# An encoder block on one core: the feed-forward norm's normed blocks in buffers apart from the squares, the squares taken by 256 columns into PSUM, and the first norm's weight loaded between the blocks

## The chip, the cores and the metric

The kernel runs on one core of a Trainium2 chip. The metric is the device time of one execution in microseconds (us), as the median of several. TensorE (PE) multiplies matrices and transposes, VectorE (DVE) and ScalarE (ACT) work element by element, GpSimd (POOL) issues the gathers of table rows and some loads, and SyncE (SP) issues nearly all other transfers. PSUM holds the results of PE, SBUF the tiles. A tile made with `bufs=N` has N buffers in turn: the N+1st waits until the first is no longer needed.

## The reference

One layer over 1024 tokens of width 1024:

```python
def rms_norm(x, g):
    y = x * lax.rsqrt(jnp.mean(x * x, axis=-1, keepdims=True) + EPS)
    return y * g

h = rms_norm(x, mix_norm_g)                    # "first norm"
proj = h @ w_in                                # u, q, k, v, f_logit, g_ssm, g_att
merged = sigmoid(g_ssm) * s5_branch(u, ...) + sigmoid(g_att) * forgetting_attention(q, k, v, f_logit, ...)
x = x + merged @ w_out                         # output projection and residual
h2 = rms_norm(x, ffn_norm_g)                   # "feed-forward norm"
x = x + peer_ffn(h2, w_query, sub_keys, u_tab, v_tab)
```

`peer_ffn` makes queries from `h2` (8 heads of 256), finds the best experts among 16384 by two sets of 128 keys, and mixes the experts' rows `u` and `v` by gates.

## The kernel before, in words

The tokens are worked on in two groups of 512 (group 0, group 1), each in NB = 4 blocks of 128. For each group the function that the diff touches does, in turn: the first norm (L470 to L489), the forget gate (weight `wf`, L496 to L507), the projections (`unit` gets a weight in two halves as `ws`; `by_token`, L460, and `by_column`, L466, multiply), the two branches, and the part named `mix` (from L822): the output projection with the residual (L838), the feed-forward norm (L843 to L851), and then the query heads (L866 on: `w_query` units with L466, keys `sk`, scores L881).

The feed-forward norm goes like this before the change. The residual L838 writes a block's 1024 columns in four strokes of 256, each from one of two PSUM banks `mm`; the strokes of one quarter of the columns come for all four blocks, then the next quarter. When a block is whole, it is stored to `d_x` (L843) and ACT squares its 1024 columns at once into a tile `sq` with two buffers, while it sums them into `ms` (L845). `inverse_root` (L431, then L150 to L155: twelve small DVE instructions with the constants) works on two blocks at a time. L850 writes the normed block, and its tile is again named `sq`: squares and normed blocks share the same two buffers. The normed block is stored to `d_h` (L851) and turned by `transposed`: eight PE transposes (L171) in two halves, each of which ACT copies (L173) and DVE splits (L174) into `h2T`. So a third normed block can be written only when the store of the first has landed.

A scheduler that simulates the engines sets each engine's order of instructions from the program; the rows below show it as it came out. Work of the next or the former part is laid in between: in group 0 the feed-forward norm stands directly ahead of group 1's first norm (its `hT`) and forget gate, and `h2T` of group 0 is stored to `d_hT` (L864, 3 MB). In group 1 the norm is followed by the loads `dhT` on POOL, the query heads, and the dense part (L1127 on, L1148 and L1208), in which all experts' rows are streamed. Ahead of group 1's norm the same engines gather expert rows for a first part of the tokens (`r`, L995, with DVE's L1001 and L1003).

SP works through its queue in order. It holds eight semaphores for landings in turn, so that a transfer there is issued only when the one eight places before it has landed.

Of the kernel before, what the change touches and what calls it, by code (L numbers as in the profile page):

```python
# [20 lines left out]
FT = mybir.dt.float32  # L21
# [4 lines left out]
AF = mybir.ActivationFunctionType  # L26
OP = mybir.AluOpType
AX = mybir.AxisListType.X
DVE, PE = mybir.EngineType.DVE, mybir.EngineType.PE

S = 1024
D = 1024
P = 128
# [24 lines left out]
def kernel(ctx: ExitStack, tc: tile.TileContext, x, w_in, w_f, w_query, w_out, w_glu,  # L58
                      g_mix, g_ffn, q_g, k_g, f_bias, a_re, a_im, log_step, b_re, b_im, c_re, c_im,
                      d_skip, sub_keys, uv, ut, out):  # L60
    nc = tc.nc
    const = ctx.enter_context(tc.tile_pool(name="const", bufs=1))
    dram = ctx.enter_context(tc.tile_pool(name="dram", bufs=1, space=bass.MemoryType.DRAM))
    psum = ctx.enter_context(tc.tile_pool(name="psum", bufs=1, space=bass.MemoryType.PSUM))
# [26 lines left out]
    def row_bcast(pool, name, src, n, parts=P):  # L91
        t = pool.tile([parts, n], FT, name=name)
        nc.sync.dma_start(t, bass.AP(tensor=src.tensor, offset=src.offset, ap=[[0, parts], [1, n]]))
        return t
# [327 lines left out]
    def front(g):  # L422
        t0, GT = GROUPS[g]
        NB, NC, B0 = GT // P, GT // L, t0 // P
# [5 lines left out]
        def inverse_root(pool, o, m):  # L430
            nc.vector.tensor_scalar(m, m, 1.0 / D, EPS, op0=OP.mult, op1=OP.add)  # L431
            rsqrt(pool, o, m)
# [38 lines left out]
        with tc.tile_pool(name=f"nrm{g}", bufs=1, side="right", reuse_waits="tile") as sp:  # L471
            xs = []
            ms = sp.tile([P, NB], FT, name="ms")
            rs = sp.tile([P, NB], FT, name="rs")
            for b in range(NB):
                xb = sp.tile([P, D], FT, name="xb", bufs=NB)
                nc.sync.dma_start(xb, x[t0 + b * P:t0 + (b + 1) * P, :])
                sq = sp.tile([P, D], FT, name="sq", bufs=NB)
                nc.scalar.activation(sq, xb, AF.Square, accum_out=ms[:, b:b + 1])
                xs.append(xb)  # L480
            gmix = row_bcast(sp, "gmix", g_mix, D)
            if g == 0:
                load_constants()
            for b in range(NB):
                if b % 2 == 0:
                    inverse_root(sp, rs[:, b:b + 2], ms[:, b:b + 2])
                hb = sp.tile([P, D], FT, name="sq", bufs=NB)
                nc.vector.scalar_tensor_tensor(hb, xs[b], rs[:, b:b + 1], gmix, op0=OP.mult, op1=OP.mult)
                transposed(hT[:, :, :, b * P:(b + 1) * P], hb)  # L489
# [120 lines left out]
        sp = ap_ctx.enter_context(tc.tile_pool(name=f"att{g}", bufs=1, side="left", reuse_waits="tile"))  # L610
# [10 lines left out]
        for hp in range(4):  # L621
# [6 lines left out]
            rs = pj.tile([P, 2, NB, 2], FT, name="rs", bufs=2)  # L628
            for qk in range(2):
                w = unit(w_in[2 + 4 * qk + hp], "att")  # L630
                raw = pj.tile([P, NB, 2, P], FT, name="qkraw", bufs=2)
                for b in range(NB):
# [3 lines left out]
                    for h in range(2):  # L636
                        sq = pj.tile([P, P], FT, name="sq")
# [184 lines left out]
        with tc.tile_pool(name=f"mix{g}", bufs=1, side="left", reuse_waits="tile") as sp:  # L822
            h2T = sp.tile([P, 8, 2, GT], FR, name="h2T")
            nx = ExitStack()
            mp = nx.enter_context(tc.tile_pool(name=f"res{g}", bufs=1, side="left", reuse_waits="tile"))
            gffn = row_bcast(mp, "gffn", g_ffn, D)
            xs = []
            for b in range(NB):
                xb = mp.tile([P, D], FT, name="xb", bufs=NB)
                nc.sync.dma_start(xb, x[t0 + b * P:t0 + (b + 1) * P, :])  # L830
                xs.append(xb)
            for q in range(4):
                w = unit(w_out[q], "out")
                cs = slice(q * 256, (q + 1) * 256)
                for b in range(NB):
                    pp = mm_bank([P, 256])
                    by_token(pp, mT, w, b, 0)
                    nc.vector.scalar_tensor_tensor(xs[b][:, cs], pp, 0.25, xs[b][:, cs],  # L838
                                                   op0=OP.mult, op1=OP.add)
            ms = mp.tile([P, NB], FT, name="ms")  # L840
            rs = mp.tile([P, NB], FT, name="rs")
            for b in range(NB):
                nc.sync.dma_start(d_x[B0 + b], xs[b])  # L843
                sq = mp.tile([P, D], FT, name="sq", bufs=2)
                nc.scalar.activation(sq, xs[b], AF.Square, accum_out=ms[:, b:b + 1])  # L845
            for b in range(NB):
                if b % 2 == 0:
                    inverse_root(mp, rs[:, b:b + 2], ms[:, b:b + 2])
                hb = mp.tile([P, D], FT, name="sq", bufs=2)
                nc.vector.scalar_tensor_tensor(hb, xs[b], rs[:, b:b + 1], gffn, op0=OP.mult, op1=OP.mult)  # L850
                nc.sync.dma_start(d_h[B0 + b], hb)  # L851
                pump(*BESIDE["norm"])
                transposed(h2T[:, :, :, b * P:(b + 1) * P], hb)
            if last_group:
                pump(0, 1000)
                gates_ctx.close()
                apart_ctx.close()
            nx.close()
            sp = nx.enter_context(tc.tile_pool(name=f"query{g}", bufs=1, side="left", reuse_waits="tile"))
            tops = [sp.tile([P, 2, H, 2, 16], FT, name="tops", bufs=NB) for _ in range(NB)]  # L860
            if last_group:
                dense_input(h2T)
            else:
                nc.sync.dma_start(d_hT, h2T[:, :, :, N1:].bitcast(FT))  # L864
            yield
            for h in range(H):  # L866
                w = unit(w_query[h], "mix")
                sk = sp.tile([P, 2, P], FT, name="sk", bufs=2)
                nc.sync.dma_start(sk, sub_keys[:, 2 * h:2 * h + 2, :])
                qs = []  # L870
                for c in range(2):
                    pq = mm_bank([P, GT])
                    by_column(pq, h2T, w, c)
                    q = sp.tile([P, GT], FT, name="q", bufs=2)
                    nc.scalar.activation(q, pq, AF.Copy)
                    qs.append(q)
                for b in range(0, NB, 2):
                    pc = tp_bank([P, 2, 2, P])
                    for bb in range(2):
                        for c in range(2):  # L880
                            nc.tensor.matmul(pc[:, bb, c, :], qs[c][:, (b + bb) * P:(b + bb + 1) * P],  # L881
                                             sk[:, c, :], start=True, stop=True)
                    sc = sp.tile([P, 2, 2, P], FT, name="sc", bufs=2)
                    nc.scalar.activation(sc, pc, AF.Copy)
                    for bb in range(2):
                        top = tops[b + bb]
                        for c in range(2):
                            top16(sc[:, bb, c, :], top[:, 0, h, c, :], top[:, 1, h, c, :].bitcast(U32))
            for b in range(NB):
                nc.sync.dma_start(d_s[B0 + b], tops[b])  # L890
            nx.close()
# [426 lines left out]
```

## Time and profile before

| | us |
|---|---|
| median of the runs | 3397.88 |
| the runs | 3397.88, 3392.59, 3992.58 |
| the profiled execution, its own time | 3395.97 |
| its span in the trace | 3394.0 |
| PE busy in the span | 3209.4 (95%) |
| DVE busy | 2587.1 (76%) |
| ACT busy | 1220.3 (36%) |
| POOL busy | 1032.7 (30%) |

The span is what the trace covers; the execution's own time is 1.97 us longer. The run of 3992.58 stands apart from the other two. The page of the profile also gives the chain of work that ended last, followed back from the last instruction: PE is 78% of it, DVE and DMA 7% each. The mean granted clock of TensorE in the profiled execution was 0.972 of full speed.

### The profile page before, as it was taken

The numbers are of one execution on the slowest core, as the hardware profiler recorded it, in microseconds if no ns is written. First come the engines' busy times: TensorE is split into PE (matmuls) and PEld (weight loads), VectorE is DVE, ScalarE is ACT, GpSimd is POOL, SyncE is SP. The second block draws the span as 40 slices with busy tenths as digits, with TensorE's granted clock in tenths as the row PEclk, the third lists the DMA queues.
The fourth block names the chain that finished last, engine by engine and source line by source line (L and its number), as shares of the span: only waits on it lengthen the run. The fifth ranks groups of instructions, "written<-read, shape, count | busy, mean of one in ns | idle before, by whom it ended". The sixth has DMA issues, their size and how long they took to land.

```text
span 3394.0 us, 51977 instructions
## 1 busy us (share of the span) xinstructions
PE 3209.4 (95%) x18959; PEld 2859.5 (84%) x18959; DVE 2587.1 (76%) x5405; ACT 1220.3 (36%) x2693; POOL 1032.7 (30%) x831
## 2 busy tenths in 40 slices
PE   7899998979999797799999999999999999999998
PEld 6788777867788686789999998988888889889887
DVE  7645454788877657578898788888988888897987
ACT  4444242323455444313774222222222222222221
POOL 0000000002222022200213365555545555564643
PEclk9999898989999998899999999999999999999999
DMA  7877996756577599945979798989989899898996
GB/s 253 284 266 278 295 330 238 278 202 227 184 227 240 137 325 336 324 175 173 256 217 320 273 362 295 348 316 333 337 309 365 323 333 345 311 348 298 359 328 230
DMA packets 465312, 965.42 MB, mean 284 GB/s; under 512 B 198304, under 2 KB 226208, under 8 KB 440480
## 3 DMA queue, kind: packets, MB, share of 16 engines
q1 hardware_dynamic: 345872, 545.43, 47.0%
q0 software_dynamic: 119184, 416.67, 34.3%
q8 instruction: 149, 2.44, 0.3%
q14 instruction: 107, 0.88, 0.1%
HBM read 775.84 MB, written 186.12 MB: 283 GB/s over the span
## 4 chain that ended last, share of the span: by engine, by line
PE 78%; DVE 7%; DMA 7%; issue 4%; ACT 2%; POOL 1%; SPq 0%; DVEq 0%; ACTq 0%; POOLq 0%
PE mm L1148 25%; PE S L1208 20%; PE mm L460 9%; PE mm L466 7%; PE tp L1208 5%; PE tp L1096 3%; PE S L692 2%; PE S L727 2%; PE S L696 1%; DMA wraw<-in_w_in_dram 1%; PE S L466 1%; POOL r L995 1%; PE tp L719 1%; DMA d_h<-sq 1%; DMA sw<-d_sc 1%
## 5 line engine op out<-in xcount | busy, mean ns | idle before, releaser
L1148 PE MATMUL mm<-dhT,us 128*128 128x320 f32 x6144 | 976.8, 310 | 5.1 <-ACT ag L1150 2.2
L1148 PEld LDWEIGHTS mm<-dhT,us 128*128 128x128 f32 x6144 | 930.3, 188 | 32.8 <-ACT ag L1150 2.6
L1208 PE MATMUL S<-vs,w 128*128 128x512 f32 x3072 | 794.0, 393 | 0.9 <-ACT vs L1205 0.9
L995 POOL DMA_INDIRECT r<-in_uv_dram,idx x384 | 481.4, 1254 | 783.4 <-DVE dots L1003 410.7
L995 POOL DMA_INDIRECT r<-in_uv_dram,second x384 | 515.6, 1343 | 602.2 <-DVE acc L1001 433.7
L1208 PEld LDWEIGHTS S<-vs,w 128*128 128x128 f32 x3072 | 565.7, 188 | 106.2 <-ACT vs L1205 1.9
L460 PE MATMUL mm<-ws,hT 128*128 128x256 f32 x3456 | 463.4, 292 | 49.1 <-ACT qkraw L635 24.2
L1001 DVE SCALAR_TENSOR_TENSOR acc<-r,dots,acc 128x1024 f32<-128x1024 f32 x384 | 492.0, 1281 | 18.9 <-DMA r<-in_uv_dram,second 17.2
L1003 DVE CUSTOM_DVE_ANT_0 r<-r,h 128x1024 f32<-128x1024 f32 x384 | 466.1, 1221 | 33.3 <-DMA r<-in_uv_dram,idx 32.6
L460 PEld LDWEIGHTS mm<-ws,hT 128*128 128x128 f32 x3456 | 439.5, 198 | 61.0 <-ACT qkraw L635 26.9
L1205 ACT ACTIVATE vs<-vraw 128x512 fp32r<-128x512 f32 x256 | 160.2, 627 | 351.5 <-DMA vraw<-in_uv_dram 226.9
L1140 ACT ACTIVATE us<-uraw 128x512 fp32r<-128x512 f32 x256 | 160.1, 627 | 304.5 <-PE mm L1148 282.3
L1208 PE MATMUL tp<-vs,w 128*128 128x512 f32 x768 | 259.5, 391 | 2.9 <-ACT vs L1205 2.9
L1141 DVE TENSOR_TENSOR us<-uraw,us 128x512 fp32r<-128x512 f32 x256 | 175.5, 687 | 100.4 <-ACT us L1140 100.1
L1150 ACT ACTIVATE ag<-mm 128x320 f32<-128x320 f32 x256 | 111.2, 435 | 347.4 <-PE mm L1148 343.5
L673 POOL DMA_DIRECT2D rk<-d_ck x16 | 9.4, 587 | 704.4 <-DVE tops L161 353.7
L1206 DVE TENSOR_TENSOR vs<-vraw,vs 128x512 fp32r<-128x512 f32 x256 | 175.6, 688 | 58.5 <-ACT vs L1205 58.3
L1082 ACT ACTIVATE two<-two,eT 128x128 f32<-128x128 f32 x640 | 201.7, 393 | 44.7 <-DVE two L1079 44.4
L466 PE MATMUL mm<-h2T,ws 128*128 128x512 f32 x768 | 183.0, 394 | 0.2 <-ACT h2T L173 0.2
L1096 PE MATMUL tp<-one,two 128*128 128x128 f32 x1280 | 172.8, 281 | 7.7 <-ACT two L1082 7.4
L1096 PEld LDWEIGHTS tp<-one,two 128*128 128x128 f32 x1280 | 164.3, 194 | 13.1 <-ACT two L1082 8.4
L1208 PEld LDWEIGHTS tp<-vs,w 128*128 128x128 f32 x768 | 143.5, 188 | 33.1 <-ACT vs L1205 3.3
(310 smaller groups left out, 3728.1 us busy)
## 6 DMA issues: line engine op xcount, KB each, us to landing
d_w<-ws SPq DMA_DIRECT2D x76, 1024.0 KB
ws<-d_w SPq DMA_DIRECT2D x76, 1024.0 KB
uraw<-in_ut_dram SPq DMA_DIRECT2D x256, 256.0 KB
vraw<-in_uv_dram SPq DMA_DIRECT2D x256, 256.0 KB
gs<-d_g SPq DMA_DIRECT2D x32, 1280.0 KB
d_g<-sg SPq DMA_DIRECT2D x40, 960.0 KB
wraw<-in_w_in_dram SPq DMA_DIRECT2D x44, 512.0 KB
d_a<-ag SPq DMA_DIRECT2D x32, 320.0 KB
```

What stands on the lines that cost most here:

```text
L460: nc.tensor.matmul(o, act[:, k, i, b * P:(b + 1) * P], w[k // 4][:, k % 4, j, :], start=(n == 0), stop=(n == 23))
L466: nc.tensor.matmul(o, w[k // 4][:, k % 4, i, c * P:(c + 1) * P], act[:, k, j, :], start=(n == 0), stop=(n == 3 * kk - 1))
L995: nc.gpsimd.indirect_dma_start(out=r, out_offset=None, in_=halves, in_offset=bass.IndirectOffsetOnAxis(ap=at, axis=0))
L1001: nc.vector.scalar_tensor_tensor(acc, r, dots[:, k:k + 1], acc, op0=OP.mult, op1=OP.add)
L1003: nc.vector.tensor_tensor_reduce(r, r, h2, 1.0, 0.0, op0=OP.mult, op1=OP.add, accum_out=dots[:, k:k + 1])
L1082: nc.scalar.activation(two[:, t, :], two[:, t, :], AF.Copy, scale=eT[:, 2, t1 + t:t1 + t + 1])
L1096: nc.tensor.matmul(pg[:, t, :], two[:, t, :], one[:, t, :], start=True, stop=True)
L1141: nc.vector.tensor_sub(us[:, :, 1, :], raw, us[:, :, 0, :])
L1148: nc.tensor.matmul(pa, parts[k // 4][:, k % 4, i, :], hT[:, k, j, ts], start=(n == 0), stop=(n == 23))
L1205: nc.scalar.activation(vs[:, 0, :], raw, AF.Copy)
L1206: nc.vector.tensor_sub(vs[:, 1, :], raw, vs[:, 0, :])
L1208: nc.tensor.matmul(out_of[b], w[:, p, b * P:(b + 1) * P], vs[:, q, :], start=(i == 0 and p == q), stop=(i == C8 - 1 and q == 1))
```

## The change

The squares get a PSUM tile `S` of 256 columns with two buffers, and are taken after each stroke of the residual, with their sums into `part` (four per block), which a DVE reduction adds up for two blocks. The normed blocks get three buffers of their own, `hb`; the fourth takes the next buffer of `xb`, that of the group's block 0 after its store to `d_x`. In the first norm the weight `gmix` is loaded after the second block and no longer after the fourth.

```diff
--- before.py
+++ after.py
@@ -475,10 +475,11 @@
             for b in range(NB):
                 xb = sp.tile([P, D], FT, name="xb", bufs=NB)
                 nc.sync.dma_start(xb, x[t0 + b * P:t0 + (b + 1) * P, :])
+                if b == 1:
+                    gmix = row_bcast(sp, "gmix", g_mix, D)
                 sq = sp.tile([P, D], FT, name="sq", bufs=NB)
                 nc.scalar.activation(sq, xb, AF.Square, accum_out=ms[:, b:b + 1])
                 xs.append(xb)
-            gmix = row_bcast(sp, "gmix", g_mix, D)
             if g == 0:
                 load_constants()
             for b in range(NB):
@@ -829,6 +830,9 @@
                 xb = mp.tile([P, D], FT, name="xb", bufs=NB)
                 nc.sync.dma_start(xb, x[t0 + b * P:t0 + (b + 1) * P, :])
                 xs.append(xb)
+            ms = mp.tile([P, NB], FT, name="ms")
+            rs = mp.tile([P, NB], FT, name="rs")
+            part = mp.tile([P, NB, 4], FT, name="part")
             for q in range(4):
                 w = unit(w_out[q], "out")
                 cs = slice(q * 256, (q + 1) * 256)
@@ -837,16 +841,15 @@
                     by_token(pp, mT, w, b, 0)
                     nc.vector.scalar_tensor_tensor(xs[b][:, cs], pp, 0.25, xs[b][:, cs],
                                                    op0=OP.mult, op1=OP.add)
-            ms = mp.tile([P, NB], FT, name="ms")
-            rs = mp.tile([P, NB], FT, name="rs")
+                    sq = psum.tile([P, 256], FT, name="S", bufs=2)
+                    nc.scalar.activation(sq, xs[b][:, cs], AF.Square, accum_out=part[:, b, q:q + 1])
             for b in range(NB):
                 nc.sync.dma_start(d_x[B0 + b], xs[b])
-                sq = mp.tile([P, D], FT, name="sq", bufs=2)
-                nc.scalar.activation(sq, xs[b], AF.Square, accum_out=ms[:, b:b + 1])
             for b in range(NB):
                 if b % 2 == 0:
+                    nc.vector.tensor_reduce(ms[:, b:b + 2], part[:, b:b + 2], axis=AX, op=OP.add)
                     inverse_root(mp, rs[:, b:b + 2], ms[:, b:b + 2])
-                hb = mp.tile([P, D], FT, name="sq", bufs=2)
+                hb = mp.tile([P, D], FT, name="hb", bufs=3) if b < 3 else mp.tile([P, D], FT, name="xb", bufs=NB)
                 nc.vector.scalar_tensor_tensor(hb, xs[b], rs[:, b:b + 1], gffn, op0=OP.mult, op1=OP.mult)
                 nc.sync.dma_start(d_h[B0 + b], hb)
                 pump(*BESIDE["norm"])
```

The lines of the changed kernel are counted on by these edits: L838 becomes L842, L843 L847, L850 L853, L851 L854, L864 L867, L496 L497, L869 L872.

On SP, in group 0, where the feed-forward norm ends; `wf` is the forget gate's weight of group 1, `sk` the first keys. Before:

```order
L843 DMA d_x_124<-xb 128x1024
L851 DMA d_h_129<-sq 128x1024
L851 DMA d_h_130<-sq 128x1024
L851 DMA d_h_131<-sq 128x1024
L851 DMA d_h_132<-sq 128x1024
L496 DMA wf<-in_w_f_dram 128x64
L869 DMA sk<-in_sub_keys_dram 128x256 x2
L864 DMA d_hT<-h2T 2048x1x384
L527 DMA d_ck<-rows 8x512 x2
```

After the change:

```order
L854 DMA d_h_129<-hb 128x1024
L854 DMA d_h_130<-hb 128x1024
L847 DMA d_x_124<-xb 128x1024
L854 DMA d_h_131<-hb 128x1024
L854 DMA d_h_132<-xb 128x1024
L867 DMA d_hT<-h2T 2048x1x384
L497 DMA wf<-in_w_f_dram 128x64
L872 DMA sk<-in_sub_keys_dram 128x256 x2
L528 DMA d_ck<-rows 8x512 x2
```

The store of `d_hT` now stands ahead of the load of `wf` and of `sk`, and the first two normed blocks are stored ahead of the last `d_x`.

On DVE, in group 1, around the last stroke of the residual (`mm` to `xb`). Before:

```order
L154 TENSOR_TENSOR rsq_t<-rsq_t,ms 128x2
L155 SCALAR_TENSOR_TENSOR rs<-rsq_t,rs 128x2
L838 SCALAR_TENSOR_TENSOR xb<-mm,xb 128x256
L850 SCALAR_TENSOR_TENSOR sq<-xb,rs,gffn 128x1024 x2
L431 TENSOR_SCALAR ms<-ms 128x2
L150 TENSOR_SCALAR rs<-ms 128x2
L174 TENSOR_TENSOR h2T<-tp,h2T 128x4x128
L153 SCALAR_TENSOR_TENSOR rsq_t<-rs 128x2
L174 TENSOR_TENSOR h2T<-tp,h2T 128x4x128
```

After the change, in the same place:

```order
L154 TENSOR_TENSOR rsq_t<-rsq_t,ms 128x2
L842 SCALAR_TENSOR_TENSOR xb<-mm,xb 128x256
L155 SCALAR_TENSOR_TENSOR rs<-rsq_t,rs 128x2
L853 SCALAR_TENSOR_TENSOR hb<-xb,rs,gffn 128x1024 x2
L842 SCALAR_TENSOR_TENSOR xb<-mm,xb 128x256
L174 TENSOR_TENSOR h2T<-tp,h2T 128x4x128
L850 TENSOR_REDUCE ms<-part 128x2
L431 TENSOR_SCALAR ms<-ms 128x2
L174 TENSOR_TENSOR h2T<-tp,h2T 128x4x128
```

The first two normed blocks now come ahead of the last stroke, and the sum of the second two blocks' squares stands behind the first split of `h2T`.

On SP, in group 1, in the same place of the program; the `ws` rows are halves of `w_query`'s units. Before:

```order
L453 DMA ws<-d_w_6294 128x2048
L453 DMA ws<-d_w_6301 128x2048
L843 DMA d_x_128<-xb 128x1024
L851 DMA d_h_133<-sq 128x1024
L851 DMA d_h_134<-sq 128x1024
L851 DMA d_h_135<-sq 128x1024
L851 DMA d_h_136<-sq 128x1024
L453 DMA ws<-d_w_6418 128x2048
L453 DMA ws<-d_w_6425 128x2048
L869 DMA sk<-in_sub_keys_dram 128x256 x2
```

After the change:

```order
L854 DMA d_h_133<-hb 128x1024
L453 DMA ws<-d_w_6321 128x2048
L453 DMA ws<-d_w_6328 128x2048
L854 DMA d_h_134<-hb 128x1024
L847 DMA d_x_128<-xb 128x1024
L854 DMA d_h_135<-hb 128x1024
L854 DMA d_h_136<-xb 128x1024
L453 DMA ws<-d_w_6445 128x2048
L453 DMA ws<-d_w_6452 128x2048
L872 DMA sk<-in_sub_keys_dram 128x256 x2
```

The first normed block's store moved ahead of a weight's two halves; the weight of the third unit and the keys stand behind all four stores, as before.

## Rows read from the trace of the kernel before

**Rows 1.** The page: busy time by engine, then the chain that ended last

```profile
PE 3209.4 (95%) x18959; PEld 2859.5 (84%) x18959; DVE 2587.1 (76%) x5405; ACT 1220.3 (36%) x2693; POOL 1032.7 (30%) x831
...
PE mm L1148 25%; PE S L1208 20%; PE mm L460 9%; PE mm L466 7%; PE tp L1208 5%; PE tp L1096 3%; PE S L692 2%; PE S L727 2%; PE S L696 1%; DMA wraw<-in_w_in_dram 1%; PE S L466 1%; POOL r L995 1%; PE tp L719 1%; DMA d_h<-sq 1%; DMA sw<-d_sc 1%
```

**Rows 2.** What PE waited for in 1575 to 3394: total us, times, longest

```profile
PE tp L1208 <- ACT vs L1205: 2.9, 1, 2.9
```

**Rows 3.** The chain that ended last, 1 to 30: start, us, what

```profile
2.60 7.82 DMA gmix<-in_g_mix_dram
...
10.75 4.10 DMA wraw<-in_w_in_dram
```

**Rows 4.** Timeline there, ACT: start, us, line, tile, idle before

```profile
14.87 1.06 ACT L447 ACTIVATE ws<-wraw 128x1024 fp32r<-128x1024 f32 x1 [3.64 <-DMA wraw<-in_w_in_dram]
```

**Rows 5.** Timeline of DVE in group 1's feed-forward norm

```profile
1411.74 0.69 DVE L174 TENSOR_TENSOR h2T<-tp,h2T 128x512 fp32r<-128x512 f32 x1
...
1412.54 0.16 DVE L154 TENSOR_TENSOR rsq_t<-rsq_t,ms 128x2 f32<-128x2 f32 x1
1412.73 0.16 DVE L155 SCALAR_TENSOR_TENSOR rs<-rsq_t,rs 128x2 f32<-128x2 f32 x1
1424.55 1.28 DVE L850 SCALAR_TENSOR_TENSOR sq<-xb,rs,gffn 128x1024 f32<-128x1024 f32 x1 [11.66 <-DMA d_h<-sq]
```

**Rows 6.** Timeline of PE in the same place

```profile
1406.87 1.09 PE L171 MATMUL tp<-idf,sq 128*128 128x128 f32 x8 [1.71 <-DVE sq L850]
...
1425.98 1.94 PE L171 MATMUL tp<-idf,sq 128*128 128x128 f32 x8 [14.91 <-DVE sq L850]
...
1430.29 21.41 PE L466 MATMUL mm<-h2T,ws 128*128 128x512 f32 x92 [0.22 <-ACT h2T L173]
```

**Rows 7.** Timeline of SyncE's queue in the same place

```profile
1412.60 15.40 SPq L851 DMA_DIRECT2D d_h<-sq  x4
1440.85 1.23 SPq L453 DMA_DIRECT2D ws<-d_w  x2
1442.17 1.51 SPq L869 DMA_DIRECT2D sk<-in_sub_keys_dram  x2
```

**Rows 8.** Stretches: busy us of PE, PEld, DVE, ACT, POOL; clock, DMA share, GB/s

```profile
560.00:568.00 8.00, 7.31 (x29) 5.28 (x28) 4.43 (x7) 3.58 (x6) 0.00 (x0) 0.50 1.03 369
...
1424.00:1436.00 12.00, 9.24 (x40) 7.23 (x41) 5.24 (x6) 2.28 (x4) 0.00 (x0) 0.77 1.30 390
1436.00:1449.00 13.00, 13.00 (x59) 10.78 (x58) 0.00 (x0) 1.20 (x2) 2.69 (x3) 1.00 1.23 360
1449.00:1452.00 3.00, 3.00 (x17) 2.53 (x17) 0.00 (x0) 0.00 (x0) 0.00 (x0) 1.00 0.20 70
```

**Rows 9.** Timeline of DVE in group 0's feed-forward norm

```profile
545.46 0.69 DVE L174 TENSOR_TENSOR h2T<-tp,h2T 128x512 fp32r<-128x512 f32 x1
...
550.67 2.48 DVE L850 SCALAR_TENSOR_TENSOR sq<-xb,rs,gffn 128x1024 f32<-128x1024 f32 x2 [4.06 <-DMA d_h<-sq]
```

**Rows 10.** Timeline of PE in the same place

```profile
540.40 1.06 PE L171 MATMUL tp<-idf,sq 128*128 128x128 f32 x8 [1.80 <-DVE sq L850]
...
566.15 0.78 PE L504 MATMUL mm<-hT,wfs 128*8 128x512 f32 x1
```

**Rows 11.** Timeline of SyncE's queue in the same place

```profile
558.17 0.58 SPq L864 DMA_DIRECT2D d_hT<-h2T  x1
```

**Rows 12.** Timeline of DVE, then of PE, where group 1's output projection begins

```profile
1347.11 1.28 DVE L1001 SCALAR_TENSOR_TENSOR acc<-r,dots,acc 128x1024 f32<-128x1024 f32 x1 [1.39 <-DMA r<-in_uv_dram,second]
...
1348.79 3.57 PE L460 MATMUL mm<-ws,hT 128*128 128x256 f32 x15 [8.60 <-DVE xb L838]
```

**Rows 13.** Groups of one line: ns min/median/max, first and last start

```profile
L845 ACT ACTIVATE sq<-xb x8: 1049/1058/1062, 530.5 to 1405.7; 128x1024 f32<-128x1024 f32 x8
L845 ACT ACTIVATION_READ_ACCUMULATOR sq<-xb x8: 184/186/193, 531.4 to 1406.7; 128x1 f32 x8
...
L537 ACT ACTIVATE ut<-mm x16: 357/383/385, 37.8 to 600.9; 128x256 f32<-128x256 f32 x16
```

## The prediction

> **What bounds the kernel now.** I read the page first. PE is busy 95% of the span, and the chain that ended last is mostly PE [rows 1]. The dense part at its end (L1148, L1208) has nothing to lose or win here: from 1575 us on PE's longest wait is 2.9 us [rows 2]. So a microsecond won or lost ahead of it passes to the end, and the question is where PE waits in the places that the change touches. There are four: the start, the feed-forward norm of group 0, the first residual of group 1, and its norm. For each I took the timelines of PE, DVE and SP's queue.
>
> In group 1's norm PE stands idle 14.91 us until the third normed block, and DVE in turn waits 11.66 us for the landing of the first block's store `d_h`, because their buffers are shared [rows 5, 6]. The store was issued at 1412.60 [rows 7], when DMA was saturated: it moves 390 and 360 GB/s up to 1449, and 70 after [rows 8]. In group 0 the same wait is only 4.06 us [rows 9]. In both norms PE also waits for the first normed block, 1.71 and 1.80 us [rows 6, 10].
>
> **The start: 0.** `gmix` is the fifth transfer in the queue before; it lands at 2.60 + 7.82 = 10.42 us, and the first norm has its first normed blocks soon after [rows 3]. After the change it is the third, and these are ready some 2.4 us sooner. But ACT's copies of the transposed blocks stand behind the first `ws` copy, which waits until 14.87 for a weight issued at 10.75 [rows 3, 4], in the changed order too. That weight is issued when the fifth transfer has landed, whichever of the five that is, and the five carry the same bytes. So the sooner block waits for the same weight: 0, with bounds of −1 (slower) and +1.5.
>
> **Squares by 256 columns: 0.** Four ACT squares of 1.06 us with a sum read of 0.19, 5.0 us per group, become sixteen. For one of 256 columns the nearest row is L537, 0.38, from PSUM to SBUF; 16 × (0.38 + 0.19) = 9.1 us [rows 13]. The added 4.1 us lie beside the matmuls of the residual, on an engine that is busy 36% [rows 1]. On the path lie only the last square and a reduction of 8 sums, some 0.2 us by the small DVE instructions [rows 5], in place of the whole 1.06 + 0.19; both are inside the next two terms. If ACT had no room the cost would be 4.1 a group.
>
> **Group 1's norm: 12.8, of which 1.5 is lost again.** The sums of the first two blocks no longer wait for a square of 1024 columns, and the order puts both of their normed blocks ahead of the last stroke of the residual. So PE's 1.71 us wait [rows 6] goes, and everything up to the last split of block 1 comes that much sooner: it ended at 1411.74 + 0.69 and now at 1410.72. Behind it stand five small DVE instructions of the second root, 0.19 apart [rows 5]: 0.97. The third normed block then starts at 1411.7, where it started at 1424.55: 12.85 sooner. It needs no store any more. The fourth, 1.28 later, writes the `xb` buffer of block 0, whose `d_x` store must have landed. That holds: the first `d_h` was issued at 1412.60 [rows 7], it stands eight places behind this store in SP's queue before, and a transfer is issued when the one eight before it has landed. Behind the normed blocks the chain is the same, so the first L466 goes from 1430.29 [rows 6] to 1417.5.
>
> What is late next: the third unit's weight and the keys. Their buffers come free with the matmuls of the first unit, so they are issued 12.8 sooner too, at 1428.0 where it was 1440.85 [rows 7]. They are needed when 96 matmuls of L466 are done. These take 21.41/92 = 0.233 each [rows 6], 22.4 together: at 1439.9. They are 2.36 MB (two halves of 1024 KB, two keys of 128 KB). From 1428 to 1449 the trace moves 8 × 390 + 13 × 360 GB/s = 7.8 MB [rows 8], these among them, the rest mainly POOL's loads and gathers. If the two queues share evenly, the weight takes 2 × 2.36 MB at 375 GB/s = 12.6 us and lands at 1440.6, with some 0.8 until PE sees it 1441.4: a loss of 1.5. If it came before all else it would lose nothing; behind all else it lands at 1449 and loses 9.1. I take 1.5, because `d_h`, which the order puts behind another weight's two halves, had landed 11.9 us after its issue [rows 5, 7], though DMA was as full there.
>
> The Trainium skill ("DMA: Bandwidth & Descriptors", section "Queues, rings and completion order") says that each engine goes round between the queue rows that have work, a packet at a time. By that rule the weight can't come behind all else: the sum would keep the 11.3, and without it 3.7 in the worst case. No row here separates the shares of the two queues.
>
> **Group 0's norm: 2.8.** By the same steps PE's 1.80 us [rows 10] go, and the last split of block 1 ends at 545.46 + 0.69 − 1.80 = 544.35. Seven small instructions (1.36) follow in the new order; the third normed block starts at 545.7 instead of 550.67 [rows 9], 5.0 sooner. It would bring L504 from 566.15 [rows 10] to 561.2, if `hT` were the last to come. But the order moves the load of `wf` behind the 3 MB store `d_hT` on SP, and L504 reads it. That store was issued at 558.17 [rows 11], and now at 553.2. At 369 GB/s [rows 8] its 3.15 MB take 8.5 us; with one us from issue to flow it is through at 562.7. Small loads behind big ones in this queue come out after them: `gmix` took 7.82 us behind four blocks [rows 3]. With the split of `wf`, 0.6 us for ACT and DVE together, L504 starts at 563.3: 2.8 sooner. The bounds are 0, if store and load take longer beside the `d_h` stores, and 5.0, if `wf` isn't held up.
>
> The Trainium skill ("DMA: Bandwidth & Descriptors", section "Two DMAs through the same engine are not ordered") says that in one queue of one engine transfers start in order, though they need not end so. By it `wf` would start when the store's last pieces have started, 2.8; without it, 5.0. The landing of `gmix` agrees with it.
>
> **The first residual of group 1: 1.0.** PE waits 8.60 us for the first L838, which stands behind a gather step L1001; that one waited 1.39 us for its row and takes 1.28 [rows 12]. In the new order the first two L838 stand ahead of it. All of it would be 2.7, but the gathers that depend on L1001 come later by as much, and the order of the gathers before is changed a little. I take 1.0, bounds 0 and 2.7.
>
> **The sum.** 0 + 0 + (12.8 − 1.5) + 2.8 + 1.0 = 15.1 us. The profiled execution took 3395.97, 1.9 below the median of 3397.88, so I forecast 3395.97 − 15.1 = 3381 us, 0.5% less. A measurement of this kernel can tell about 2% (68 us) from no change; all cases lie well within. With the terms at moderate ends this case runs from 3376 to 3387. Chance 0.50.
>
> **Rivals.** *The DMA backlog takes most of it back.* The weight and keys land only when the backlog is through: 12.8 − 9.1 + 2.8 + 1.0 = 7.5, so 3388.5. For it speaks that DMA runs full from 1424 to 1449 [rows 8]; against it, that the load is issued 12.8 us sooner. Chance 0.22.
>
> *Everything comes free.* `wf` isn't held up, the weight comes in time, L1001 costs its whole 2.7: 12.8 + 5.0 + 2.7 = 20.5, so 3375.5. Chance 0.12.
>
> *The change doesn't do what it says.* The wait moves to another buffer: the fourth block waits for the store of `d_x` as the third did for `d_h`, and group 1 wins nothing. 2.8 + 1.0 remain: 3392. The issue at 1412.60 speaks against it. Chance 0.08.
>
> *Slower.* The scheduler laid the gathers ahead of group 1's norm a little differently. There DVE and POOL go hand in hand, and a step that meets a row not yet landed stops PE for as much as the 8.60 us seen at 1340 to 1349 [rows 12]. Two more such waits, 17.2, undo the gain (3398); from the second on it is slower, and three give 3395.97 − 15.1 + 25.8 = 3407. Against it: the number of gathers and their order on POOL hardly differ. Chance 0.08.
>
> **How the numbers follow.** The range has to reach from the case with everything free, less the 1.5 of the start and a few us between executions, to the case in which group 1 wins nothing: 3371 to 3394. Left out are the slower case and the edges. No case comes near 2% either way, so "within 2%" has 0.98, and 0.01 for each side.
>
> **What would show it.** In the profile after, group 1's third normed block should start near 1411.7 + the shift so far, with no wait for `d_h`, L466 some 12.8 us sooner beside it, and a new wait of PE at L881 or L466 for the keys or the weight of 1 or 2 us (9 in the first rival). In group 0 L504 should wait for `wfs`. Squares on ACT should take 0.38 us or less. The first L504 should be at 28.4 as before. Wrong would make it a long wait in the gathers, a fourth block that waits for `d_x`, or a keys' landing past 1445.

## The result and the profile after

The changed kernel takes 3378.76 us (median of 8 executions, 3372.07 to 3382.76), the kernel before 3400.32 beside it; the ratio is 0.9942, with a 95% interval of 0.9931 to 0.9952, so 16 to 23 us less of 3400 (the two medians alone give 0.9937, which lies in the interval). The forecast was 3381, the range 3371 to 3394. The profiled execution took 3382.74 us with a span of 3380.8, and lies among the slower of its eight; that of the kernel before took 3395.97 and lies among its faster ones. The two traces are therefore only 13.2 us apart; a second pair of traced executions (3391.44 and 3381.50) is 9.9 apart.

DVE's timeline in the norm of group 1, after the change (start, us, line, tile, idle before); it answers to [rows 5]:

```profile
1398.44 2.48 DVE L853 SCALAR_TENSOR_TENSOR hb<-xb,rs,gffn 128x1024 f32<-128x1024 f32 x2
...
1404.81 0.69 DVE L174 TENSOR_TENSOR h2T<-tp,h2T 128x512 fp32r<-128x512 f32 x1
1406.39 1.29 DVE L853 SCALAR_TENSOR_TENSOR hb<-xb,rs,gffn 128x1024 f32<-128x1024 f32 x1
1407.59 1.28 DVE L853 SCALAR_TENSOR_TENSOR xb<-xb,rs,gffn 128x1024 f32<-128x1024 f32 x1
```

The third and fourth normed blocks follow without a wait for any store; the 11.66 us are gone. PE's timeline there, which answers to [rows 6], with the end of the residual's matmuls ahead of it and the first keys' scores behind:

```profile
1397.84 2.92 PE L460 MATMUL mm<-ws,hT 128*128 128x256 f32 x23
1400.60 1.03 PE L171 MATMUL tp<-idf,hb 128*128 128x128 f32 x8
1402.61 0.66 PE L171 MATMUL tp<-idf,hb 128*128 128x128 f32 x4 [0.98 <-DVE h2T L174]
...
1407.82 1.94 PE L171 MATMUL tp<-idf,hb 128*128 128x128 f32 x8 [3.68 <-DVE hb L853]
...
1412.12 3.04 PE L466 MATMUL mm<-h2T,ws 128*128 128x512 f32 x9
...
1434.74 1.95 PE L884 MATMUL tp<-sk,q 128*128 128x128 f32 x16
```

The transposes start where the residual's matmuls end, so the 1.71 us are gone as well, and the long wait has shrunk from 14.91 to 3.68 us. From the end of the residual's last matmul (1397.84 + 2.92 = 1400.76) to the first L466 it is 11.36 us, where it was 1430.29 − 1405.16 = 25.13 (the end of before's last matmul stands with the version with the buffers alone, below). SP's queue, which answers to [rows 7]:

```profile
1411.21 0.54 SPq L854 DMA_DIRECT2D d_h<-xb  x1
1423.15 1.23 SPq L453 DMA_DIRECT2D ws<-d_w  x2
1424.48 0.85 SPq L872 DMA_DIRECT2D sk<-in_sub_keys_dram  x2
```

The third unit's weight and the keys are issued 17.7 us sooner (4.4 of them because the residual itself ends sooner by that), and the scores at 1434.74 wait for neither.

In group 0 the chain of waits and the queue show what holds the gate. The chain first (start, us, what), then SP's queue, then PE:

```profile
551.70 0.58 SPq L867
...
552.33 10.36 DMA wf<-in_w_f_dram
562.77 0.27 ACT wfs L499
```

```profile
551.70 0.58 SPq L867 DMA_DIRECT2D d_hT<-h2T  x1
552.33 3.01 SPq L497 DMA_DIRECT2D wf<-in_w_f_dram  x1
```

```profile
557.43 1.26 PE L171 MATMUL tp<-idf,sq 128*128 128x128 f32 x8 [0.81 <-DVE hT L174]
563.08 1.02 PE L505 MATMUL mm<-hT,wfs 128*8 128x512 f32 x2 [4.38 <-ACT wfs L499]
```

The gate starts at 563.08, where it started at 566.15 [rows 10]; PE stands 4.38 us for a weight of 32 KB that lands 10.4 us after its issue, behind the 3 MB store.

### The profile page after: what moved, and what is told of

Read it like the earlier page. It is cut to its first block, busy times and chain, and to the rows that moved or that the text cites. A ratio compares the mean times of both kernels' runs of the same rounds, so it can differ in the third digit from the quotient of the medians.

```text
span 3380.8 us, 52031 instructions
## 1 busy us (share of the span) xinstructions
PE 3211.6 (95%) x18959; PEld 2861.4 (85%) x18959; DVE 2588.7 (77%) x5409; ACT 1226.0 (36%) x2741; POOL 1035.3 (31%) x831
## 4 chain that ended last, share of the span: by engine, by line
PE 79%; DVE 9%; DMA 8%; ACT 2%; issue 2%; SPq 1%; POOL 0%; DVEq 0%; ACTq 0%; POOLq 0%
PE mm L1151 25%; PE S L1211 20%; PE mm L460 9%; PE mm L466 8%; PE tp L1211 5%; PE tp L1099 3%; PE S L466 2%; PE S L728 2%; PE S L693 1%; DMA wraw<-in_w_in_dram 1%; DMA vraw<-in_uv_dram 1%; PE S L697 1%; PE tp L720 1%; DVE r L1006 1%; DVE tops L161 1%
## 5 line engine op out<-in xcount | busy, mean ns | idle before, releaser
L466 PE MATMUL mm<-h2T,ws 128*128 128x512 f32 x768 | 183.4, 395 | 0.0
```

The lines of the kernel that those rows point to most:

```text
L466: nc.tensor.matmul(o, w[k // 4][:, k % 4, i, c * P:(c + 1) * P], act[:, k, j, :], start=(n == 0), stop=(n == 3 * kk - 1))
```

## The experiments

For each version that the text compares, this table gives five stretches worked out from its trace: (a) from the residual's last matmul of group 0 to the gate of group 1 (L504/L505), (b) from there to group 1's first residual stroke on DVE, (c) from there to the last matmul of that residual, (d) the norm of group 1 up to the first L466, (e) from there to the end of the span. Two numbers are two traces of the same kernel.

| | a | b | c | d | e | ratio to before (95%) |
|---|---|---|---|---|---|---|
| before | 27.6, 28.9 | 782.2, 781.5 | 56.9, 56.5 | 25.1, 25.4 | 1963.7, 1962.7 | 1 |
| changed | 24.4, 25.2 | 781.8, 784.3 | 55.9, 55.7 | 11.4, 11.4 | 1968.7, 1963.5 | 0.9942 (0.9931 to 0.9952) |
| gmix back | 25.8, 24.5 | 789.5, 783.7 | 56.0, 55.9 | 11.4, 11.4 | 1966.8, 1968.3 | 0.9949 (0.9936 to 0.9962) |
| buffers alone | 24.7, 24.7 | 776.1, 773.5 | 55.8, 56.6 | 11.8, 11.8 | 1968.6, 1968.4 | 0.9935 (0.9916 to 0.9953) |
| squares alone | 27.1, 27.4 | 776.0, 776.1 | 56.9, 57.0 | 22.2, 22.0 | 1969.7, 1966.6 | 0.9970 (0.9960 to 0.9979) |
| changed, wf kept | 21.3 | 781.1 | 55.7 | 11.6 | 1966.9 | 0.9914 (0.9898 to 0.9930) |
| the same, gmix back | 21.0 | 777.1 | 56.4 | 11.5 | 1967.0 | 0.9912 (0.9892 to 0.9932) |
| stores by ScalarE | 26.8 | 783.7 | 55.6 | 13.6 | 1967.1 | 0.9964 (0.9954 to 0.9974) |
| buffers alone, wf kept | 21.4 | 774.4 | 55.8 | 11.8 | 1972.2 | 0.9930 (0.9914 to 0.9947) |

**Buffers alone.** On the kernel before:

```diff
-                sq = mp.tile([P, D], FT, name="sq", bufs=2)
+                sq = mp.tile([P, D], FT, name="sq", bufs=1)
...
-                hb = mp.tile([P, D], FT, name="sq", bufs=2)
+                hb = mp.tile([P, D], FT, name="hb", bufs=2) if b < 2 else mp.tile([P, D], FT, name="xb", bufs=NB)
```

> The kernel before, with normed blocks apart from the squares alone: squares 1024 wide in one buffer, the first two normed blocks in two buffers of their own, the third and fourth in the xb buffers of blocks 0 and 1. Theory (the wait for the first block's store carries the gain): no wait of DVE for d_h in either group, group 1's third normed block 11 to 13 us sooner, PE's 1.7 us wait ahead of the first transposes still there; 13 to 16 us under the kernel before. Rival (the squares and the order that comes with them carry it): 5 us or less under it. Second rival (the wait moves to the stores of d_x, whose buffers two blocks now take): DVE waits for d_x by some us, 5 to 10 us under it.

The time is as the changed kernel's: some 22 us under the kernel before (16 to 29 by the interval), more than the 13 to 16 of the theory. The norm of group 1 takes 11.8 us, and there is no wait for `d_x` either. Its PE timeline in group 1's norm:

```profile
1387.81 4.48 PE L460 MATMUL mm<-ws,hT 128*128 128x256 f32 x36
1392.39 1.06 PE L171 MATMUL tp<-idf,hb 128*128 128x128 f32 x8
...
1399.75 1.94 PE L171 MATMUL tp<-idf,xb 128*128 128x128 f32 x8 [4.07 <-DVE xb L850]
```

One thing was expected otherwise: PE's 1.71 us ahead of the first transposes are gone here too, with squares 1024 wide. They did not come from the width of the squares. PE, DVE and ACT in the kernel before, where the residual's last matmul ends (1399.04 + 6.12 = 1405.16):

```profile
1399.04 6.12 PE L460 MATMUL mm<-ws,hT 128*128 128x256 f32 x49
...
1405.19 0.42 DVE L838 SCALAR_TENSOR_TENSOR xb<-mm,xb 128x256 f32<-128x256 f32 x1 [1.40 <-PE mm L460]
1405.54 2.64 DVE L850 SCALAR_TENSOR_TENSOR sq<-xb,rs,gffn 128x1024 f32<-128x1024 f32 x2
...
1405.71 1.06 ACT L845 ACTIVATE sq<-xb 128x1024 f32<-128x1024 f32 x1 [1.73 <-DVE xb L838]
```

And DVE with the buffers alone:

```profile
1390.95 2.48 DVE L850 SCALAR_TENSOR_TENSOR hb<-xb,rs,gffn 128x1024 f32<-128x1024 f32 x2
1393.35 0.42 DVE L838 SCALAR_TENSOR_TENSOR xb<-mm,xb 128x256 f32<-128x256 f32 x1
```

Before, the first normed block did not wait for the last square, which begins 0.17 us after it; it stood behind the last stroke in DVE's order. Only the second normed block takes the buffer of the last square. With buffers of their own both are laid ahead of the last stroke, here with squares 1024 wide, and in the changed kernel and the version with the squares alone too. In the two kernels of this text with shared buffers (before, and the stores by ScalarE) they stand behind it. That the shared buffer made the scheduler choose that order is argued from this, not tried by itself.

**Squares alone.** The changed kernel with `gmix` in its old place and

```diff
-                hb = mp.tile([P, D], FT, name="hb", bufs=3) if b < 3 else mp.tile([P, D], FT, name="xb", bufs=NB)
+                hb = mp.tile([P, D], FT, name="hb", bufs=2)
```

> The changed kernel with two buffers for all four normed blocks, and gmix loaded behind all four blocks: of the change only the squares by 256 columns into PSUM are left. Theory: DVE waits again for the landing of the first block's store, some 11 us in group 1 and 4 in group 0, PE's wait ahead of the first transposes is gone; 2 to 5 us under the kernel before. Rival (the squares carry the gain): 12 us or more under it.

With the squares in PSUM the two buffers belong to the normed blocks alone, so this version parts them from the squares as well; what it leaves out is the third buffer and the turn to `xb`. DVE waits for the stores again, in group 1 twice:

```profile
1408.98 1.28 DVE L852 SCALAR_TENSOR_TENSOR hb<-xb,rs,gffn 128x1024 f32<-128x1024 f32 x1 [4.39 <-DMA d_h<-hb]
1418.02 1.28 DVE L852 SCALAR_TENSOR_TENSOR hb<-xb,rs,gffn 128x1024 f32<-128x1024 f32 x1 [4.31 <-DMA d_h<-hb]
```

SP's queue there tells why the waits are shorter than the 11.66 us of before:

```profile
1403.97 0.60 SPq L853 DMA_DIRECT2D d_h<-hb  x1
1404.66 2.47 SPq L453 DMA_DIRECT2D ws<-d_w  x2
1407.23 0.43 SPq L853 DMA_DIRECT2D d_h<-hb  x1
```

The first store, issued ahead of a weight's two halves, had landed by 1408.98, 5.0 us later; the second, issued behind them, by 1418.02, 10.8 later. One more thing lies between the two: POOL's 3 MB load `dhT`, issued at 1406.34. By the profile's list of DMA queues it matters less; `q1` is the queue of SP here, `q0` that of POOL, and the line gives packets, MB and the share of the 16 engines from 1407.23 to 1418.02:

```profile
q1 hardware_dynamic: 563, 3.09, 86.5%
q0 software_dynamic: 322, 0.49, 16.2%
```

The norms win 0.9 (a) and 3.2 us (d), in the means of both traces. But the ratio says 7 to 14 us, more than the theory gave and less than the rival. The difference stands in column b, a stretch in which neither kernel was edited.

**The stretch between the gate and the residual.** Is that the execution or the kernel? Five kernels were traced a second time:

> The kernel before once more, for a second trace. Theory (the stretch from group 1's gate to its output projection, 782 us in the first trace, differs between executions of one kernel by some us): it comes out 3 to 8 us from 782, with the norm stretches within 0.5 us of the first trace. Rival (it is set by the order of instructions, and so by the kernel): 782 within 1.

> The version with the squares alone once more, for a second trace. Theory (the stretch from group 1's gate to its output projection differs between executions): it comes out some us from the 776 of its first trace. Rival (it is set by the kernel's order, and gives this version some 6 us that the norms don't): 776 within 1.

> The changed kernel once more, for a second trace. Theory (the order of instructions sets the stretch from group 1's gate to its output projection): 781.8 us again within 1, group 1's norm 11.4 again. Rival (it differs by execution): 3 us or more from it.

> The version with gmix loaded behind all four blocks once more, for a second trace. In its first trace the stretch from group 1's gate to its output projection took 789.5 us, 7.7 more than in the changed kernel, and that execution was the slowest of five, 11 us over their median. Theory (the 789 is of that execution): 780 to 784 here. Rival (it is of this version's order): 789 within 2.

> The version with the buffers alone once more, for a second trace. Theory (its order of instructions gives the stretch from group 1's gate to its output projection 776 us, 6 less than the kernel before): 776 within 2, and the norm of group 1 11.8. Rival (the 6 us are of that execution): 780 or more.

The kernel before repeats within 0.6 us in b (its column a differs by 1.4, more than the 0.5 expected of the norms) and the squares alone within 0.1: for these two the theory that b is a matter of the execution falls. The changed kernel (2.5 apart) lies between both expectations. The buffers alone came to 773.5, 2.6 apart, a little outside the theory's 2 and far from the rival's 780. With `gmix` back the 789.5 was of that execution, as expected. Read together: b belongs in part to the version, 773 to 776 in the four traces of the buffers alone and the squares alone and 781 to 784 in most others, and an execution adds up to 3 us, once 6. The traces show the order of every engine's instructions in b. It is the same in the kernel before and with the stores by ScalarE (782.2, 781.5, 783.7), the same in the changed kernel and with `gmix` back (781.8, 784.3, 789.5, 783.7), and, but for its two ends, the same in the two versions with the weight kept from the changed kernel (781.1 and 777.1, 4 us apart); in the others it differs. So the order is a likely cause of the 6 us between versions, but no run changed the order alone. For the change itself b is worth nothing that shows: 782 before and 782 to 784 after.

**Stores by ScalarE.** The kernel before with

```diff
-                nc.sync.dma_start(d_h[B0 + b], hb)
+                nc.scalar.dma_start(d_h[B0 + b], hb)
```

> The kernel before, with the four stores of normed blocks issued by ScalarE instead of SyncE; buffers, squares and gmix as before. Theory (the first block's store lands late because it stands behind a weight's two halves in SyncE's queue): DVE's wait for d_h in group 1 falls from 11.7 us to 3 to 5, and 5 to 9 us of the gain come without a buffer more. Rival (it lands late because the transfers are saturated whoever issues them): the wait stays above 9 us, the time within 3 us of the kernel before.

ACT's queue and DVE in group 1's norm:

```profile
1407.21 0.33 ACTq L851 DMA_DIRECT2D d_h<-sq  x1
```

```profile
1405.90 2.64 DVE L850 SCALAR_TENSOR_TENSOR sq<-xb,rs,gffn 128x1024 f32<-128x1024 f32 x2
1413.39 1.28 DVE L850 SCALAR_TENSOR_TENSOR sq<-xb,rs,gffn 128x1024 f32<-128x1024 f32 x1 [0.77 <-DMA d_h<-sq]
```

The rival falls: of the 11.66 us wait 0.77 is left, less than the theory's 3 to 5, and the norm takes 13.6 us without a buffer more. The kernel before has the store at 1412.60, for 11.86 us in its chain of waits; from SP's queue and that chain:

```profile
1410.09 1.91 SPq L453 DMA_DIRECT2D ws<-d_w  x2
...
1412.60 11.86 DMA d_h<-sq
```

There it was issued 7.4 us after the residual's end (1405.16), behind a weight's two halves and a `d_x`. Here it was issued 1.7 us after it (1405.54) and had landed at most 6.2 later. So half of what was won (5.7 us) is the sooner issue, and half the shorter flight (5.7). The shorter flight is no proof of a quicker queue: this store was issued ahead of the weight, as the 5.0 us store above, and the one of before behind it, as the 10.8 us one. SP's queue in this version:

```profile
1410.63 2.58 SPq L453 DMA_DIRECT2D ws<-d_w  x2
```

The list of queues tells more. ACT's queue is `q10`, which only this version has. From 1407.21 to 1411.20 and from 1414.80 to 1419.10 it doesn't appear. All packets there are those of SP's queue, in the first stretch many small ones, in the second few large ones:

```profile
q1 hardware_dynamic: 3431, 0.89, 85.1%
...
q1 hardware_dynamic: 222, 1.22, 96.8%
```

So the first store, issued at 1407.21, moved nothing for 4.0 us. The third was issued by ACT at 1414.70, behind the weight, and moved nothing for at least 4.4, although its own queue had sent off the two stores ahead of it (1.05 MB from 1411.20 to 1414.80):

```profile
1414.70 0.33 ACTq L851 DMA_DIRECT2D d_h<-sq  x1
```

A queue of its own did not carry the third store past what SP had issued. The first one ACT could issue while SP was held up at a `d_x` (1406.29 to 1410.54), and so ahead of the weight; whether the other queue helped it beside that, this run doesn't separate. The time fell by 9 to 16 us.

The Trainium skill ("DMA: Bandwidth & Descriptors", section "Issuing engines are not separate DMA queues") says that issuing from several engines "will only save the time on the sequencer it takes to initiate the DMA". The run agrees as to what is saved: SP's sequencer stood at its own transfers, and ACT's did not. It was not small here: 11.4 us between the residual's end and the store's landing, half of it in the flight of a store that now came ahead of the weight.

**gmix back.** The changed kernel with the old place of `gmix`:

```diff
-                if b == 1:
-                    gmix = row_bcast(sp, "gmix", g_mix, D)
...
+            gmix = row_bcast(sp, "gmix", g_mix, D)
             if g == 0:
```

> The changed kernel, with the first norm's weight gmix loaded behind all four blocks again. Theory (the sooner gmix wins nothing and costs about 1 us at the start, which the trace has lost again by 504 us): the first L505 back at 28.4 instead of 29.4, the time the same as the changed kernel's within 1 us, some 20 us under the kernel before. Rival (the sooner gmix is part of the gain): 1 to 3 us slower than the changed kernel.

The time cannot be told from the changed kernel's, nor can those of the two versions with the kept weight from each other. The first gate starts at 28.5 and 28.2 us in its two traces, in the changed kernel at 29.4 and 28.9. So the sooner `gmix` costs some 0.5 to 1 us there and wins nothing.

**The gate's weight kept.** The changed kernel with

```diff
+    wfs = const.tile([P, 8, 2, H], FR, name="wfs")
...
-            wf = sp.tile([P, 8, H], FT, name="wf")
-            nc.sync.dma_start(wf, w_f)
-            wfs = sp.tile([P, 8, 2, H], FR, name="wfs")
-            nc.scalar.activation(wfs[:, :, 0, :], wf, AF.Copy)
-            nc.vector.tensor_sub(wfs[:, :, 1, :], wf, wfs[:, :, 0, :])
+            if g == 0:
+                wf = sp.tile([P, 8, H], FT, name="wf")
+                nc.sync.dma_start(wf, w_f)
+                nc.scalar.activation(wfs[:, :, 0, :], wf, AF.Copy)
+                nc.vector.tensor_sub(wfs[:, :, 1, :], wf, wfs[:, :, 0, :])
```

> The changed kernel, with the forget gate's split weight loaded and split once, for group 0, and kept for group 1, so that nothing is loaded behind the store of d_hT that the gate needs. Theory (the load behind the store holds up group 1's gate): PE's 4.4 us wait for wfs goes, L505 starts near 559 instead of 563; 3 to 5 us faster than the changed kernel, 23 to 25 under the kernel before. Rival (another transfer that stands behind the store is late next, or PE's matmuls behind it wait for a weight): the same as the changed kernel within 1 us.

> The changed kernel with the forget gate's split weight kept from group 0 and gmix loaded behind all four blocks: the version that the runs so far point to. Theory: the gate of group 1 has nothing to wait for, the norm of group 1 keeps its 13.7 us; 20 to 28 us under the kernel before, within 3 of the version with the sooner gmix. Rival (the start or the stretch behind the gate gives it back): 17 us or less under it, like the changed kernel.

The gate follows the last transposes at once:

```profile
556.71 1.73 PE L172 MATMUL tp<-idf,sq 128*128 128x128 f32 x8 [0.56 <-DVE hT L175]
558.51 0.40 PE L506 MATMUL mm<-hT,wfs 128*8 128x512 f32 x1
```

Column a falls from 24.4 and 25.2 to 21.3 and 21.0: 3 to 4 us, as expected. Both versions beat the changed kernel (0.9914 and 0.9912; their intervals end about where its interval begins), by some 10 us, more than these 4 and, for the first, more than the 3 to 5 of its theory. Of the rest, column b holds 2 us in the one and 6 in the other, which no edit explains; the remainder the traces don't show.

> The kernel before, with the normed blocks apart from the squares (squares 1024 wide in one buffer, as in the version with the buffers alone) and the forget gate's split weight kept from group 0; no squares in PSUM, gmix as before. Theory (buffers and the kept weight are all that carries; the squares by 256 columns are worth nothing beside them): gate 21 us after group 0's residual, group 1's norm 11.5 us, time 20 to 30 us under the kernel before, as the version with everything (0.991). Rival (the squares are needed for it): 5 us or more slower than that version, with PE waiting ahead of the first transposes again.

With the squares left 1024 wide and in SBUF, a is 21.4 and d 11.8, as with everything; the ratio, 0.9930, doesn't tell this version from the changed kernel nor clearly from the two above (the intervals overlap). So the squares in PSUM are worth nothing that shows beside the buffers, at most the 0.2 to 0.4 us of column d.

## Why the prediction was right

**Group 1's norm: right, mis-sized by 1.** The forecast was 12.8 us sooner, for the reason given, the first block's store; measured are 25.1 − 11.4 = 13.8 (25.4 − 11.4 = 14.0 in the second pair). The third block starts 1406.39 − 1400.76 = 5.63 us after the residual, where it was 1424.55 − 1405.16 = 19.39. About half of the extra 0.9 is in the second eight of the first sixteen transposes, which took 1.97 us before and 1.54 after; the rest is steps of 0.1 to 0.2. The windows of the sixteen, in the kernel before, after the change and with the stores by ScalarE (busy us of PE, PEld, DVE, ACT, POOL; granted clock, DMA share, GB/s):

```profile
1406.80:1411.20 4.40, 3.06 (x16) 2.43 (x16) 3.67 (x12) 1.83 (x5) 0.00 (x0) 0.76 0.84 221
```

```profile
1400.60:1404.00 3.40, 2.20 (x18) 1.63 (x16) 2.67 (x10) 2.08 (x5) 0.00 (x0) 1.00 0.94 283
```

```profile
1407.20:1411.00 3.80, 2.40 (x16) 1.69 (x16) 3.54 (x11) 1.87 (x5) 0.00 (x0) 1.00 0.86 222
```

Before, PE had stood 1.71 us ahead of them, and for a part of the window the clock was granted at its lower level (1.2 GHz), a mean of 0.76; now they follow the matmuls at once and stay at 2.4 GHz. But that wait alone does not bring the lower clock: with the stores by ScalarE PE stood 1.71 us in the same place, and the clock stayed at 1.00. One attribution in this step was wrong in part: beside the order, the 1.71 us were put down to the squares' width; the version with the buffers alone shows that they go with squares 1024 wide, by the order that comes with separate buffers.

**What is lost again: 1.5 forecast, for a wait that did not come.** PE waits neither for the keys nor for the weight. Its first dense matmul follows the first L466 by 105.0 and 104.8 us, where it was 103.7 and 104.4: 0.9 more in the means, which nothing ties to the weight or the keys, with 0.7 between the two traces of before. The 0.8 us from a landing until PE sees it, which the term counts in, stands in no row; in group 0 `wfs` starts 0.1 us after the landing of `wf`. The rival with the backlog (9.1 lost) is out: the weight was issued 11.6 us ahead of the scores and was there.

**Group 0's norm: right, in part by luck.** The forecast said 2.8, with `wf` held up behind `d_hT` until about 562.7 and the gate at 563.3; the trace has 562.77 and 563.08. Column a gives 3.2 for the first pair of traces, 3.5 for the means of both pairs. The mechanism is the forecast one: taking the load away gave 3 to 4 us more, where 2.2 were worked out (5.0 − 2.8). But both sizes were low and cancel: without the hold-up the gate comes 7.1 us sooner in the means (28.2 − 21.2), not 5.0. Store and load took 11.0 us from the store's issue to the landing of `wf` (551.70 to 562.69), not 9.5 (the one us in it, from issue to flow, stands in no row); and the store was issued 1.5 sooner than forecast. With this the rival in which everything comes free is out as well.

**Squares: right at 0.** ACT's timeline in group 0 after the change, one of sixteen:

```profile
521.98 0.39 ACT L845 ACTIVATE S<-xb 128x256 f32<-128x256 f32 x1 [1.39 <-DVE xb L842]
522.31 0.19 ACT L845 ACTIVATION_READ_ACCUMULATOR S<-xb 128x1 f32 x1
```

0.39 + 0.19 as bounded from L537 [rows 13], with ACT idle ahead of it.

**The start: 0 forecast, 0.3 to 1.0 lost.** ACT's first weight is there at 15.22 instead of 14.87 [rows 4]:

```profile
15.22 1.06 ACT L447 ACTIVATE ws<-wraw 128x1024 fp32r<-128x1024 f32 x1 [3.03 <-DMA wraw<-in_w_in_dram]
```

So the bound weight came 0.35 us later, not at the same time. This is within the bound of −1. At the end of group 0's residual the first pair of traces shows nothing of it (538.7 against 538.6); in the second pair that end comes at 539.5 against 534.5, so what becomes of it can't be told.

**The first residual of group 1: the step that failed.** It was worth 1.0 in the sum. PE's wait for the first stroke did become shorter, 7.69 instead of 8.60 us [rows 12]:

```profile
1345.35 6.93 PE L460 MATMUL mm<-ws,hT 128*128 128x256 f32 x43 [7.69 <-DVE xb L842]
```

In the second pair of traces it is 7.81 instead of 9.08, so the step was right about the wait. But the whole stretch b is no shorter, 782 to 784 against 782: what the wait gave, the stretch ahead of it took. The forecast names such a cost, the changed order of the gathers before, but gives it no price of its own. The residual itself (c) is 0.8 us shorter, 55.8 against 56.7 in the means; this was not foreseen, its cause was not tried, and two traces of the version with the buffers alone are as far apart.

**The sum.** Terms read from the means of both traces: d 13.9, a 3.5, c 0.8, less 0.7 at the start, less 1.2 in b, less 0.9 up to the dense part: 15.4, against 15.1 forecast, with a ratio that says 16 to 23. Beside them the traced executions differ by up to 5 us in stretches that no term speaks of (in the means 1.9 lost from the first gate to group 0's residual, 2.1 from the dense part on), so that the traced spans are 13.2 and 9.9 apart and not 15.4. That the sum comes so near 15.1 is luck in part: the terms for the residual and for the lost wait did not come as forecast, and c, group 0's extra 0.7 and the extra 1.1 of group 1's norm filled their place. One part of e was found: in the first trace of the changed kernel the clock falls in the dense part where it did not before.

```profile
1557.00:1565.00 8.00, 8.00 (x44) 8.00 (x45) 7.41 (x14) 1.71 (x4) 1.35 (x1) 0.79 0.64 215
```

At 0.79 of full speed 8 us lose 1.7. It falls again behind PE's wait of 2.9 us near the end [rows 2], and there in the kernel before too, but for longer now; before, then after:

```profile
3354.00:3366.00 12.00, 9.14 (x33) 7.04 (x33) 8.40 (x10) 1.26 (x2) 4.20 (x4) 0.86 1.02 375
```

```profile
3340.00:3352.00 12.00, 9.11 (x28) 7.23 (x28) 7.53 (x9) 1.26 (x2) 2.94 (x4) 0.72 1.03 402
```

So the dense part has a little to lose after all, by the clock and not by a wait. What makes the medians differ by some us more than the traced pairs do stays open.

**The rivals.** The wait did not move to another buffer: the fourth block starts 1.20 us after the third, with no wait for `d_x`. The slower rival had a point in its size: the stretch of the gathers, b, differs by some 6 us between versions in which it was not edited, though downwards and not up, and whether by waits for gathered rows was not looked into. That it came to nothing for this change is luck; the forecast had no row from which to know it.

## What to carry to other kernels

A temporary that shares its buffers with a result that is stored makes the next result wait for the store, and the store for whatever stands ahead of it in its queue; a buffer of its own takes that wait away. To issue the store from an engine that isn't held up took away nearly all of it too, here with the store ahead of a weight's two halves and no longer behind them. When a wait on the path goes, look at what the new order puts in front of the next small load: 32 KB behind 3 MB cost as much as the change had won in that norm. A version's time holds some us that come from stretches it did not edit: compare stretch by stretch before a difference of half a per cent is put down to an edit.

## What the runs showed of the hardware that was not expected

Two stores of 512 KB in one queue, 3.3 us apart, landed 5.0 and 10.8 us after their issue; between them two 1 MB loads were issued in that queue, and a 3 MB load in POOL's, which moved 0.49 MB by the second landing against 3.09 in theirs. A store issued by ScalarE behind the same two loads of SyncE moved no packet for at least 4.4 us, with nothing else waiting in its own queue. Behind an idle time of PE of 1.71 us the granted clock fell within sixteen transposes in the kernel before (a mean of 0.76) and stayed at 1.00 in the version with the stores by ScalarE.
